# The first stage of a two-block network by pairs of K-blocks, with its early modulation in pieces of 256 columns

## The chip, the cores and the metric

The kernel runs on one core of one Trainium2 chip. The metric is the device time of one execution in microseconds (us), as the median of several runs of the same program; lower is better. A core has five engines that run their own instruction streams: TensorE (PE in the profile, with its weight loads apart as PEld), VectorE (DVE), ScalarE (ACT), GpSimd (POOL) and SyncE (SP), which here issues all loads from memory.

## The reference

Two blocks of layers over 256 tokens of width 1024, batch 1. What matters here is the beginning of the first layer, which treats the sequence `x` and a context `ctx` of 256 tokens alike:

```python
mod   = silu(c)     @ w_ada[0] + b_ada[0]        # 6*1024 columns: sh1, sc1, g1, sh2, sc2, g2
mod_c = silu(c_ctx) @ w_ada[0] + b_ada[0]
h  = rms_norm(x,   norm_mix[0]) * (1 + sc1)  + sh1
hc = rms_norm(ctx, norm_mix[0]) * (1 + sc1c) + sh1c
b_gate, c_gate, u = split(h @ conv_w_in, 3)      # 3 x 1024 columns; the same for hc
y = (b_gate * conv3(c_gate * u)) @ conv_w_out    # three taps along the tokens
```

The rest of the layer (gates g1 and g2, a SwiGLU layer), an attention layer and a second block of four feed-forward layers and two mixers follow. All of it is computed in float32 accuracy.

## The kernel before

Activations lie transposed: 128 features on the partitions, `KB` = 8 blocks of 128 features ("K-blocks"), and 512 columns, 256 tokens of x beside 256 of ctx. A float32 product is made of three matmuls of a faster type: each operand is split into a high part (rounded, by ScalarE) and a low part (the rest, by VectorE), and `mm3` (L241) adds high x high, high x low and low x high in one PSUM bank. In the profile these three are L243, L244 and L245.

Weights come as a stream of units (`WeightStream`, L67). A unit is up to 1024 columns per partition, here 2 K-blocks x 512 columns or 4 K-blocks x 256 columns (512 KB). There are 5 raw buffers, into which SP loads the units in the order of `stream_specs` (L698), and 4 buffers each for the high and the low parts. `take` (L111) splits up to two units ahead of the one it hands out (L106 on ScalarE, L107 on VectorE, in pieces of 512 columns); a load waits until its raw buffer has been split, or for an unsplit unit until it has been used.

Each engine executes its instructions in a fixed order. This order is made when the program is built: it follows the text, but an instruction whose inputs the builder takes to be ready may be put ahead of others that are not. So the text below gives priorities rather than the exact order.

The first stage is in `conv_block` (L759). X and ctx are loaded (L1784, L802), squared and summed (`squares`, L341), and `diagonal` makes the statistics: 8 matmuls against a vector of 1/D per 256 tokens (L361), a chain of some ten small VectorE steps that ends in the reciprocal root, and a diagonal matrix (L782). `normalise` spreads it over the partitions with one matmul (L787) and multiplies (L789), into `xr`.

The modulation vectors of the first layer's shift and scale are 2048 columns, made in four chunks of 512 (`ADA_FIRST`: chunks 0, 2, 1, 3; chunks 0 and 1 are the shift, 2 and 3 the scale). For all four chunks the 2 or 4 columns of silu(c) are the stationary operand and the weights move. Chunks 0 and 2 go by `ada_direct` (L446): the raw float32 weights, 8 matmuls of 512 columns each (L455). Chunks 1 and 3 go by `ada_fast` (L409): split weights against split silu columns, 16 matmuls of 512 columns each (L418, L419). The result is a row of 512 columns on 2 or 4 partitions; it is copied out of PSUM by ScalarE (L460, L424), turned into columns by four small transposes (L441, L428), and the bias is added (L444, or L432 to L435).

With chunks 0 and 2 the shift and scale of K-blocks 0 to 3 are there, and `modulate(0)` makes these four blocks of the convolution's input: `mod_scale` (L515), then for each block two ScalarE instructions (L798), a cast and a subtraction (L251, L252 into `xh` and `xl`). PE then adds these four K-blocks for the first four output blocks (two of c_gate, two of u, `pcu`). Chunks 1 and 3 and `modulate(1)` give the other four K-blocks. The two output blocks of b_gate follow with all eight K-blocks (L842). Group 0 is thus 6 output blocks x 8 K-blocks x 3 = 144 matmuls of 512 columns; three more groups like it follow. After each group VectorE and ScalarE take the banks out: a copy (L847), the product (L849), the three taps (L851 to L853), the gate (L855) and a split. Then `ada_at` starts the modulation of a later piece by VectorE alone (`ada_slow`, L476 and L478).

PSUM has 8 banks. `banks(5, 3)` (L194) makes 5 main banks for the blocks and 3 auxiliary banks, which the statistics, the spread diagonal and the modulation use. A bank is handed on tile by tile.

## Time and profile before

| what | us |
|---|---|
| runs (3): median | 2060.99 |
| runs: lowest and highest | 2060.79, 2061.44 |
| the profiled execution | 2061.66 |
| its span, first to last instruction | 2059.9 |
| TensorE busy in the span | 2022.4 |
| VectorE busy | 1522.6 |
| ScalarE busy | 1062.4 |

The page of the profile has the busy time of each engine, first over the span and then in slices. The trace behind it can be asked for busy time in chosen stretches, for instructions in order of time, for groups of instructions by tile or line, and for who waited for whom. A line of the order of time reads: start, duration, engine, line of the code, operation, written tile <- read tiles, shape, count, and in brackets how long the engine stood idle before it and what ended that. Where several equal instructions follow one another they are one line, and its duration runs from the first start to the last end. Loads are attributed to SP's queue. The granted clock is the share of full speed that TensorE got.

### The profile page before, as it was taken

To read this page: it belongs to the slowest core of one execution; us is meant where nothing else is said; L and a number is where in the kernel's file an instruction comes from. 1 tells how busy PE (TensorE), PEld (TensorE's weight loads), DVE (VectorE), ACT (ScalarE), POOL (GpSimd) and SP (SyncE) were. 2 spreads that over 40 slices of the span, in tenths; PEclk is the share of its full clock that TensorE was granted. 3 is DMA by queue.
4 is the path that set the end of the run, shared out by engine and by line. 5 is a ranking of instruction groups with operands and counts; after the bars stand their busy time and mean duration, and the time that the engine had idled before them with its cause. 6 is when DMAs were issued, how large, how long until landed. Compare 5 with 4: busy or idle time off the path is not lost. (4 is left out here: it accounts for less than half of the span.)

```text
span 2059.9 us, 32409 instructions
## 1 busy us (share of the span) xinstructions
PE 2022.4 (98%) x12430; PEld 1776.4 (86%) x12430; DVE 1522.6 (74%) x2796; ACT 1062.4 (52%) x1763; POOL 4.1 (0%) x24
## 2 busy tenths in 40 slices
PE   7999999999999999999999999999999999999999
PEld 3888887888899999888888889998888888989888
DVE  6979998766377778766677667787767776887774
ACT  4534533323355566555455546555545554675552
POOL 0000000000000000000000000000000000000000
PEclk9999999999999999999999999999999999999999
DMA  7746566656254324466566564556656656425554
GB/s 249 230 144 195 174 206 197 219 189 200 89 165 148 98 88 137 138 186 188 180 190 186 178 189 137 151 171 189 189 176 192 185 183 190 138 83 166 186 180 133
DMA packets 327434, 350.93 MB, mean 170 GB/s; under 512 B 12592, under 2 KB 301488, under 8 KB 327280
## 3 DMA queue, kind: packets, MB, share of 16 engines
q1 hardware_dynamic: 327280, 348.88, 54.8%
q8 instruction: 97, 1.59, 0.3%
q14 instruction: 57, 0.47, 0.1%
HBM read 347.78 MB, written 1.05 MB: 169 GB/s over the span
## 5 line engine op out<-in xcount | busy, mean ns | idle before, releaser
L106 ACT CAST whi<-wraw 128x512 fp32r<-128x512 f32 (+1 forms) x803 | 617.0, 791 | 713.0 <-issue 245.4
L107 DVE TENSOR_TENSOR wlo<-wraw,whi 128x512 fp32r<-128x512 f32 (+1 forms) x803 | 709.5, 900 | 343.5 <-ACT whi L106 340.5
L306 PE MATMUL pg<-x,whi 128*128 128x512 f32 x1408 | 387.9, 397 | 0.5 <-DVE x L255 0.3
L306 PEld LDWEIGHTS pg<-x,whi 128*128 128x128 f32 x1408 | 241.0, 188 | 33.9 <-DVE x L255 2.8
L306 PE MATMUL po<-s,whi 128*128 128x512 f32 x880 | 243.0, 394 | 0.0
L308 PEld LDWEIGHTS pg<-x,wlo 128*128 128x128 f32 x1408 | 215.1, 188 | 31.8
L308 PE MATMUL pg<-x,wlo 128*128 128x256 f32 x1408 | 223.3, 280 | 0.0
L243 PE MATMUL pm<-xh,whi 128*128 128x512 f32 (+1 forms) x576 | 217.2, 381 | 2.8 <-ACT xh L251 2.8
L244 PE MATMUL pm<-xl,whi 128*128 128x512 f32 (+1 forms) x576 | 218.4, 380 | 0.0
L245 PE MATMUL pm<-xh,wlo 128*128 128x512 f32 (+1 forms) x576 | 217.9, 379 | 0.0
L478 DVE SCALAR_TENSOR_TENSOR ada_acc<-wraw,sil,ada_acc 128x512 f32<-128x512 f32 x224 | 159.6, 751 | 24.0 <-DMA wraw<-in_w_ada 22.6
L306 PEld LDWEIGHTS po<-s,whi 128*128 128x128 f32 x880 | 148.7, 189 | 18.0
L308 PEld LDWEIGHTS po<-s,wlo 128*128 128x128 f32 x880 | 137.5, 188 | 20.5
L308 PE MATMUL po<-s,wlo 128*128 128x256 f32 x880 | 142.5, 280 | 0.0
L243 PEld LDWEIGHTS pm<-xh,whi 128*128 128x128 f32 x576 | 109.1, 190 | 25.7 <-ACT xh L251 4.1
L244 PEld LDWEIGHTS pm<-xl,whi 128*128 128x128 f32 x576 | 109.5, 190 | 20.6 <-DVE xl L252 0.2
L245 PEld LDWEIGHTS pm<-xh,wlo 128*128 128x128 f32 x576 | 109.2, 190 | 20.5
L245 PE MATMUL pm<-sh,wlo 128*128 128x256 f32 (+1 forms) x384 | 119.3, 311 | 0.7 <-DVE wlo L107 0.7
L243 PE MATMUL pm<-sh,whi 128*128 128x256 f32 (+1 forms) x384 | 119.2, 311 | 0.0
L244 PE MATMUL pm<-sl,whi 128*128 128x256 f32 (+1 forms) x384 | 118.9, 310 | 0.0
L245 PE MATMUL pm<-whi,xl 128*128 128x256 f32 x352 | 99.7, 283 | 0.0
L306 PE MATMUL pg<-xh,whi 128*128 128x512 f32 x352 | 96.1, 394 | 0.0
(435 smaller groups left out, 3467.4 us busy)
## 6 DMA issues: line engine op xcount, KB each, us to landing
wraw<-in_ffn_w_in SPq DMA_DIRECT2D x264, 512.0 KB, 3.6
wraw<-in_ffn_w_out SPq DMA_DIRECT2D x128, 512.0 KB, 3.5
wraw<-in_w_ada SPq DMA_DIRECT2D x96, 512.0 KB, 4.5
wraw<-in_a_w_in SPq DMA_DIRECT2D x28, 512.0 KB, 3.8
wraw<-in_conv_w_in SPq DMA_DIRECT2D x24, 512.0 KB, 4.7
wraw<-in_attn_w_qkv SPq DMA_DIRECT2D x24, 512.0 KB, 4.0
wraw<-in_conv_w_out SPq DMA_DIRECT2D x16, 512.0 KB, 4.3
wraw<-in_ffn_w_out SPq DMA_DIRECT2D x28, 256.0 KB, 2.7
```

The lines of the kernel that those rows point to most:

```text
L106: self.nc.scalar.copy(hi[:, cs], raw[:, cs])
L107: self.nc.vector.tensor_tensor(lo[:, cs], raw[:, cs], hi[:, cs].bitcast(F32), ALU.subtract)
L243: mm(ps, ah, bh, start=first, stop=False)
L244: mm(ps, ah, bl, start=False, stop=False)
L245: mm(ps, al, bh, start=False, stop=last)
L306: self.nc.tensor.matmul(pss[c], hi[:, kk, cs], x2[:, done + kk], start=done + kk == 0, stop=False)
L308: self.nc.tensor.matmul(pss[c][:, 0, :], lo[:, kk, cs], x2[:, done + kk, 0, :], start=False, stop=done + kk == nblocks - 1)
L478: nc.vector.scalar_tensor_tensor(accs[v], w[:, kk, :], c, accs[v], ALU.mult, ALU.add)
```

## The change

The four chunks of 512 columns become four pieces, one for each pair of K-blocks: 256 columns of the shift and the 256 columns of the scale that belong to them.

- Piece 0 (`ada_whole`) has its weights loaded outside the stream, into two tiles of 8 x 256 columns. Here the raw float32 weights are the stationary operand and the two silu columns move: 4 column blocks x 8 K-blocks = 32 matmuls, whose results lie on the partitions already, so that only the bias is added.
- Pieces 1 to 3 (`ada_parts`) go as `ada_fast` did, with 32 matmuls of 256 columns each, in place of 16 of 512.
- The convolution of group 0 goes by pairs: for each pair of K-blocks, the six output blocks (c_gate, u, b_gate, two each) are all advanced by these two K-blocks, in six banks that stay open over the four pairs. Its units are 2 K-blocks x 256 columns (256 KB). In the text, the next piece's matmuls stand behind the pair's c_gate blocks, its copy, transposes and `modulate` behind the first u block.
- PSUM is `banks(6, 2)` until group 0 is taken out, then `banks(5, 3)` as before.
- X is the first load, ahead of the two tables `pack` and `consts`. Then come half of piece 0, ctx, the other half of piece 0, and five units of the stream (before: two units, ctx, and the others as buffers came free).

```diff
-        self.banks(5, 3)
+        self.banks(6, 2)
+        self.X = self.cp.tile([P, KB, T], F32, name="X")
+        self.load_halves(self.X, a["xT"])
         self.pk = self.cp.tile([P, NPACK], F32, name="pk")
...
+    def mod_blocks(self, i):
+
+        m = self.mod[:, 0, 0:16, :].rearrange("p (s b) v -> p s b v", s=2)[:, :, 2 * i : 2 * i + 2, :]
+        bias = self.p("b_ada0")[:, 0:16].rearrange("p (s b) -> p s b", s=2)[:, :, 2 * i : 2 * i + 2]
+        return m, bias[:, :, :, None].to_broadcast([P, 2, 2, 2])
+
+    def ada_whole(self, w):
+
+        sil = self.sil.rearrange("p (v k) -> p k v", v=2)
+        ps = self.aux_bank()
+        m, bias = self.mod_blocks(0)
+        for s in range(2):
+            for c in range(2):
+                o = 4 * s + 2 * c
+                for kb in range(KB):
+                    self.nc.tensor.matmul(ps[:, o : o + 2], w[s][:, kb, c * P : (c + 1) * P], sil[:, kb, :], start=kb == 0, stop=kb == KB - 1)
+                if c == 0:
+                    yield
+            self.nc.vector.tensor_tensor(m[:, s], ps[:, 4 * s : 4 * s + 4].rearrange("p (b v) -> p b v", b=2), bias[:, s], ALU.add)
+
+    def ada_parts(self, i):
 
         nc = self.nc
         ps = self.aux_bank()
+        for s in range(2):
+            o = ps[0:4, s * 256 : (s + 1) * 256]
+            for h in range(2):
+                hi, lo, nk, _ = self.ws.take()
+                for kk in range(nk):
+                    kb = 4 * h + kk
+                    nc.tensor.matmul(o, self.c4[:, kb, :], hi[:, kk, :], start=kb == 0, stop=False)
+                    nc.tensor.matmul(o, self.c4[:, kb, :], lo[:, kk, :], start=False, stop=kb == KB - 1)
         row = self.tmp()
         nc.scalar.copy(row[0:4, :], ps[0:4, :])
         yield
         pt = self.aux_bank()
         for b in range(4):
             nc.tensor.transpose(pt[:, 4 * b : 4 * b + 4], row[0:4, b * P : (b + 1) * P], self.ident[0:4, 0:4])
...
+        m, bias = self.mod_blocks(i)
+        for s in range(2):
+            nc.vector.tensor_tensor(m[:, s], cv[:, s, :, :, 0], cv[:, s, :, :, 1], ALU.add)
+            nc.vector.tensor_tensor(m[:, s], m[:, s], bias[:, s], ALU.add)
...
+CONV_COLS = (1024, 2048, 0)
...
-    for i in range(2):
-        s += ada_units(w[0], ADA_FIRST[i], ADA_FIRST[i] in ADA_DIRECT)
-    for k0 in (0, 4):
-        for c0 in (1024, 2048):
-            s += cols_units(a["conv_w_in"], c0, 256, k8[k0 : k0 + 4])
-        if k0 == 0:
-            for i in range(2, 4):
-                s += ada_units(w[0], ADA_FIRST[i], ADA_FIRST[i] in ADA_DIRECT)
+    for i in range(4):
+        for n, c0 in enumerate(CONV_COLS):
+            s += cols_units(a["conv_w_in"], c0, 256, k8[2 * i : 2 * i + 2])
+            if n == 0 and i < 3:
+                for c1 in (0, 1024):
+                    s += cols_units(w[0], c1 + (i + 1) * 256, 256, k8)
...
+    w0 = [ep.tile([P, KB, 256], F32, name=f"ada{s}") for s in range(2)]
...
-    net.ws.load(2)
-    net.load_halves(net.C, net.a["ctxT"])
+    for s in range(2):
+        net.load_halves(w0[s], net.a["w_ada"][0][:, 1024 * s : 1024 * s + 256])
+        if s == 0:
+            net.load_halves(net.C, net.a["ctxT"])
+    net.ws.load(5)
+    ada = net.ada_whole(w0)
     dx = diagonal(0)
-    units(0, 2)
+    next(ada)
     normalise(0, dx)
     dc = diagonal(1)
-    units(0, 2)
+    next(ada)
     normalise(1, dc)
-    units(1, 4)
-    units(0, 1)
-    units(1, 1)
+    for _ in ada:
+        pass
     modulate(0)
...
+    pcu = [[net.main_bank() for _ in range(2)] for _ in CONV_COLS]
+    for i in range(4):
+        ada = None
+        for n, pss in enumerate(pcu):
+            hi, lo, nk, _ = net.ws.take()
+            for c in range(2):
+                cs = slice(c * P, (c + 1) * P)
+                for kk in range(nk):
+                    kb = 2 * i + kk
+                    net.mm3(pss[c], hi[:, kk, cs], lo[:, kk, cs], xh[:, kb, :], xl[:, kb, :], kb == 0, kb == KB - 1)
+                if n == 1 and c == 0 and ada is not None:
+                    for _ in ada:
+                        pass
+                    modulate(i + 1)
+            if n == 0 and i < 3:
+                ada = net.ada_parts(i + 1)
+                next(ada)
     early.close()
...
+                if g == 0:
+                    net.banks(5, 3)
                 net.ada_at("conv", g)
```

More of the change, by code (lines that the diff above doesn't have):

```diff
@@ L444, in ada_columns @@
         self.nc.vector.tensor_tensor(m, pt[:, :8].rearrange("p (b v) -> p b v", b=4), bias, ALU.add)
-    def ada_direct(self, layer, j):
-        nc = self.nc
-        ps = self.aux_bank()
-        sil = self.sil.rearrange("p (v k) -> p k v", v=2)
-        done = 0
-        while done < KB:
-            w, _, nk, _ = self.ws.take()
-            for kk in range(nk):
-                nc.tensor.matmul(ps[0:2, :], sil[:, done + kk, :], w[:, kk, :], start=done + kk == 0, stop=done + kk == KB - 1)
-            done += nk
-            if done < KB:
-                yield
-        row = self.tmp()
-        nc.scalar.copy(row[0:2, :], ps[0:2, :])
-        yield
-        self.ada_columns(layer, j, row)
     def ada_slow(self, layer, j, vecs):
@@ L667, in ffn_pairs @@
         self.ws.width = 512
-ADA_FIRST = (0, 2, 1, 3)
-ADA_DIRECT = (0, 2)
+CONV_COLS = (1024, 2048, 0)
 ADA_AT = {
@@ L767, in conv_block @@
     early = ExitStack()
-    xr = early.enter_context(tc.tile_pool(name="xr", bufs=1)).tile([P, KB, 512], F32, name="xr")
-    chunk = {j: net.ada_direct(0, j) if j in ADA_DIRECT else net.ada_fast(0, j) for j in ADA_FIRST}
-    def units(i, n):
-        for _ in range(n):
-            next(chunk[ADA_FIRST[i]], None)
+    ep = early.enter_context(tc.tile_pool(name="early", bufs=1))
+    xr = ep.tile([P, KB, 512], F32, name="xr")
+    w0 = [ep.tile([P, KB, 256], F32, name=f"ada{s}") for s in range(2)]
     def diagonal(v):
@@ L790, in normalise, with modulate @@
                                     R[:, None, :].to_broadcast([P, 2, T]), ALU.mult)
-    def modulate(half):
-        net.mod_scale(0, 0, half)
+    def modulate(i):
+        net.mod_scale(0, 0, i, 2)
         a = net.modA[:, 0, :, :]
-        for kb in range(4 * half, 4 * half + 4):
+        for kb in (2 * i, 2 * i + 1):
             t = net.tmp()
```

63 lines of the change are left out of this document (17 added, 46 removed).

## The prediction

> **What bounds the kernel now.** I read the page's head first, then busy time by stretches of the span, then the order of time up to 80 us, the only part that the diff touches.
>
> ```profile
> span 2059.9 us, 32409 instructions
> PE 2022.4 (98%) x12430; PEld 1776.4 (86%) x12430; DVE 1522.6 (74%) x2796; ACT 1062.4 (52%) x1763; POOL 4.1 (0%) x24
> ```
> ```profile
> 0.00:37.70 37.70, 22.65 (x64) 7.18 (x64) 20.40 (x60) 13.11 (x26) 0.21 (x4) 0.95 0.83 272
> 37.70:77.30 39.60, 39.59 (x170) 28.76 (x171) 34.09 (x61) 28.19 (x54) 0.00 (x0) 0.96 0.69 222
> ```
>
> PE is busy for 98% of the span. The second fence (columns: stretch, length, then busy time of PE, PEld, DVE, ACT and POOL, then granted clock, DMA share, GB/s) shows that up to 37.7 us PE has 15 us idle, and that from there it is never idle. All later stages are the same code. So the change is worth what it does to one moment: the time at which PE has done the 144 convolution matmuls of group 0 (6 output blocks x 8 K-blocks x 3) and the matmuls of the four early modulation chunks. That moment now:
>
> ```profile
> L243 PE MATMUL pm<-xh,whi x49: 387/389/796, 37.7 to 79.7; 128*128 128x512 f32 x49
> ```
>
> The 49th of the L243 matmuls, the first beyond the 48 of group 0, starts at 79.7 and each step of three takes 0.7, so the moment is about 79.1 us. (Some matmuls of other groups may be among the 49; the count of work is the same.) What set the start at 37.7 is in the order of time:
>
> ```profile
> 8.71 1.15 ACT L347 ACTIVATE t<-X 128x512 f32<-128x512 f32 x2 [0.27 <-DMA X<-in_xT]
> ...
> 10.92 1.87 PE L361 MATMUL pa<-mean,acc 128*128 128x1 f32 x8 [10.92 <-DVE acc L352]
> ...
> 14.37 1.15 ACT L347 ACTIVATE t<-C 128x512 f32<-128x512 f32 x2 [0.34 <-DMA C<-in_ctxT]
> ...
> 14.99 0.48 DVE L782 TENSOR_SCALAR t<-kc,rcol 128x128 f32<-128x128 f32 x2
> ...
> 15.91 2.29 DVE L352 TENSOR_TENSOR acc<-acc,t 128x512 f32<-128x512 f32 x3
> ...
> 18.22 0.70 PE L787 MATMUL pa<-t,ones 128*128 128x256 f32 x2
> ...
> 18.75 0.95 PE L361 MATMUL pa<-mean,acc 128*128 128x1 f32 x8
> 18.95 2.48 DVE L789 TENSOR_TENSOR xr<-X,pa 128x512 f32<-128x512 f32 x4 [0.76 <-PE pa L787]
> ...
> 24.84 2.48 DVE L789 TENSOR_TENSOR xr<-C,pa 128x512 f32<-128x512 f32 x4 [0.85 <-PE pa L787]
> ...
> 33.34 0.62 ACT L106 CAST whi<-wraw 128x512 fp32r<-128x512 f32 x1 [0.92 <-DMA wraw<-in_w_ada]
> ...
> 33.86 0.57 ACT L460 COPY t<-pa 2x512 f32<-2x512 f32 x1
> ...
> 34.48 0.58 PE L441 MATMUL pa<-kc,t 2*128 2x2 f32 x4 [2.38 <-ACT t L460]
> ...
> 35.56 1.59 ACT L798 ACTIVATE t<-xr,mod,modA 128x256 f32<-128x256 f32 x3 [0.61 <-DVE modA L515]
> ...
> 37.06 0.60 ACT L251 CAST xh<-t 128x512 fp32r<-128x512 f32 x1
> ...
> 37.72 2.08 PE L243 MATMUL pm<-xh,whi 128*128 128x512 f32 x4 [0.85 <-ACT xh L251]
> ```
>
> The normalised data xr is complete at 27.3, ten us before the first convolution matmul. The last thing to come is the second modulation chunk: its row copy (L460, 33.86), transposes, the first L798. So the chunks bind the start, and half of all modulation (4.2 MB of weights) must pass before it.
>
> **The change, part by part.** *Loads.* SP now issues X (1.05 MB), pack and consts (0.54), the first 256 columns of the shift (1.05), C (1.05), the first 256 columns of the scale (1.05), then five stream units (0.26 and 4 x 0.52), none of which waits for a buffer.
>
> ```profile
> 14.00:16.00 2.00, 2.00 (x3) 0.25 (x2) 1.72 (x9) 1.17 (x3) 0.00 (x0) 1.00 1.05 386
> ```
>
> C's end has the same 3.7 MB up to it as before, so it lands at 14.3 as now (the second squares start at 14.37). At 386 GB/s the scale's columns land 2.7 later, at 17.1, the first convolution unit at 17.8, the four units of the next piece at 19.1, 20.5, 21.8 and 23.2. X no longer has 0.54 MB ahead of it: 1.4 earlier, so its second half is there at 7.3.
>
> *Modulation of pair 0 with stationary weights.* 32 matmuls, fp32 128x128 loads and two moving columns. The nearest rows are the two L361 rows, fp32 128x128 loads with one moving column: 0.23 each in one, 0.12 in the other. That is 16 x 0.23 = 3.7 after 17.1, so 20.8 at the dear end, and the additions and L515 end near 21.5. No row copy, no transposes. It lies beside the ctx chain, which ends later, so it costs nothing; if C came 5 us earlier it would be what is late.
>
> *What is late next: xr of ctx.* x: sums at 9.5 (now 10.9), L361 to 11.4, then as now from 12.8 to 15.5 the small DVE steps, so 14.1; L787 0.7 and xr from 14.9. The ctx sums (from 15.5, 2.29 of DVE) and the x normalisation (2.48) now fall on the same engine: together done at 14.9 + 4.8 = 19.7. There are two auxiliary banks instead of three, one of them held by the modulation sums, so the ctx statistics (L361) also wait until xr of x has read its bank; that wait ends inside the same 19.7. Behind it on PE stand only modulation matmuls. From L361 to xr of ctx now takes 18.75 to 24.84, 6.1, and up to 0.9 more if its eight matmuls run at 0.23; then 0.7 for the first xr piece: 26.5 to 27.4. One L798 (0.53) and one cast (0.6) with their hand-overs, 1.25: the first convolution matmul at 27.7 to 28.7. I take **28.0**, so the start comes **9.7 earlier**.
>
> *PE work behind the start.*
>
> ```profile
> 50.76 0.40 PE L419 MATMUL pa<-wlo,c 128*4 128x512 f32 x1
> 51.00 0.39 PE L418 MATMUL pa<-whi,c 128*4 128x512 f32 x1
> ...
> 54.30 0.41 PE L428 MATMUL pa<-kc,t 4*128 4x4 f32 x4
> ...
> 217.20 0.28 PE L243 MATMUL pm<-sh,whi 128*128 128x256 f32 x1
> 217.32 0.28 PE L244 MATMUL pm<-sl,whi 128*128 128x256 f32 x1
> ```
>
> The convolution matmuls are the same 144. Before, 28 of the 32 L418/L419 matmuls lie behind the start, at 0.235 from start to start: 6.6, and two sets of transposes, 0.8: 7.4. After, each of three pieces has 32 matmuls of 256 columns at 0.12: 3.8. Piece 1 (landed 19.1 to 23.2, split before the start but for the last unit, since the four split buffers also hold the first convolution unit) leaves 8 x 0.12 = 1.0; pieces 2 and 3 are 7.7; transposes 3 x 0.41 = 1.2. Sum 9.9, so **2.5 more**. If none of piece 1 ran early it would be 5.3 more, if all did, 1.5.
>
> *The pair boundaries.* Each later pair's input follows from its piece: last matmul, row copy, transposes, six small DVE steps, two L798, cast. The trace has this chain once, between busy neighbours:
>
> ```profile
> 53.08 0.39 PE L419 MATMUL pa<-wlo,c 128*4 128x512 f32 x1
> 53.51 0.58 ACT L424 COPY t<-pa 4x512 f32<-4x512 f32 x1
> ...
> 59.30 0.53 PEld L243 LDWEIGHTS pm<-xh,whi 128*128 128x128 f32 x3 [0.26 <-ACT xh L251]
> ```
>
> From 53.47 to 59.30 it takes 5.8. In the written order 24 convolution matmuls of pair i stand behind the piece:
>
> ```profile
> 66.35 0.39 PE L243 MATMUL pm<-xh,whi 128*128 128x512 f32 x1
> 66.58 0.39 PE L244 MATMUL pm<-xl,whi 128*128 128x512 f32 x1
> ```
>
> At 0.23 they cover 5.4. So PE waits about 0.5 at each of three boundaries, **1.5**. Between zero (the piece's matmuls need no xh and may run earlier) and, in the rival below, 2.4 each. The transposes wait for the row copy with 6 convolution matmuls (1.4) in front of them; behind them on PE stand the next convolution matmuls, so a late copy holds up those.
>
> *The clock.* The start itself falls in a slow stretch now, and I leave it the same after:
>
> ```profile
> 33.50:34.00 0.50, 0.00 (x0) 0.00 (x0) 0.01 (x1) 0.50 (x2) 0.00 (x0) 0.79 0.95 287
> ...
> 37.70:40.70 3.00, 2.98 (x7) 2.41 (x8) 1.38 (x2) 3.00 (x7) 0.00 (x0) 0.51 0.68 264
> ```
>
> PE stood idle for 2.38 us before 34.48. In the half microsecond from 33.5 to 34, inside that gap, the granted clock is no longer 1.00 but 0.79 on the mean, and the first 3.0 us of convolution ran at 0.51, a loss of 1.5. The Trainium skill (TensorE: Matmul & The Clock Gate, "Why this matters for your kernels") asks for no idle gaps over about 3 us, since one idle window halves the clock. By that rule a gap of 2.4 us would go unpunished, which this trace contradicts; by it the third rival's price would lack its clock part and come out at 2061.
>
> *Edits at nothing.* The bank switch to (5, 3) after group 0: group 1 opens on banks 0 and 1, which L847 frees while the last 24 matmuls still run; if not, 0.6 for a copy. Six banks for group 0 remove a wait for a bank that PE does not show now.
>
> **Sum.** -9.7 + 2.5 + 1.5 = -5.7. The profiled execution took 2061.66 (span 2059.9 and 1.76 around it) and would take 2055.9; the median of the runs lies 0.67 below it, so **2055.3**.
>
> **Rivals.** *VectorE becomes the bound.*
>
> ```profile
> 60.00:100.00 40.00, 40.00 (x178) 32.97 (x177) 39.79 (x64) 17.59 (x33) 0.00 (x0) 1.00 0.67 204
> ```
> ```profile
> L107 DVE TENSOR_TENSOR wlo<-wraw,whi 128x512 fp32r<-128x512 f32 x32 | 20.8, 690 | 6.3 <-ACT whi L106 6.2
> ```
>
> DVE has no idle time from 60 to 100. Three split pieces instead of two chunks add 4 units x 2 x 0.69 = 5.5 to it, and PE arrives 5.7 earlier. If DVE's splits then bind, PE gives back 5.5: 2060.8. For it: that row. Against it: PE is never idle there now, and much of that DVE work is the slow modulation of later pieces, which nothing in group 1 waits for.
>
> *The start comes late.* The order on an engine is fixed: L460 above stood behind a cast that waited 0.92 for its DMA. If casts of the new units stand ahead of L798 or of the ctx squares in the same way, and the start is at 32, the sum is -1.7: 2059.3.
>
> *The boundaries are late and the clock falls (slower).* Each piece needs four units through four split buffers, while up to three of them hold convolution units of the pair that is still running. If the wait at each of three boundaries reaches the 2.38 us that halved the clock above, each costs 2.4 + 1.5: 11.7 in place of 1.5, so +4.5: 2065.5. It decides from the idle time at which the clock falls: at 1.4 (33.5 less 32.1, the gap's start) three waits with their slow stretches make 8.7, more than the 7.2 that start and PE work leave. For it: three serial chains where there were two. Against it: 12.5 us of PE work per pair (36 x 0.23 + 3.8 + 0.4) stand against 2.9 MB, 7.5 us of DMA at 386 GB/s, and PE did not wait through the chain at 53 to 59 now.
>
> **How the numbers follow.** Forecast 0.67 (0.64 faster by over 0.2%, 4.1 us, about what a measurement of this kernel can tell from no change; 0.03 within it); VectorE 0.12 and late start 0.10, both within 0.2%; boundaries 0.11, slower. So faster 0.64, same 0.25, slower 0.11. The forecast's own range: start 27.7, all of piece 1 early, no boundary waits, no slow stretch (-1.5): -10.0 - 1.5 + 1.5 = -10.0, so 2051.0; start 28.7, 24 of its 32 early, waits of 1 each: -9.0 + 2.5 + 3.0 = -3.5, so 2057.5. With the two middle rivals, and half a microsecond on either side for the spread of the runs (2060.79 to 2061.44), the range is 2050.5 to 2061.3; the slower one is left out.
>
> **What would show it.** Right: first L243 on pm near 28, L361 of ctx near 20, the 48 matmuls of each line done near 73, PE full from 28 on. Start late: first L243 past 31, with ACT L106 waiting for DMA in front. Boundaries: PE idle on ACT xh L251 near 37, 48 and 60, and granted clock 0.5 after it. VectorE: PE idle on wlo L107 or on banks between 72 and 100. Wrong altogether: a first matmul near 37, or the gain there at 80 us and gone by the end.

## The result, and the profile after

| | median us | lowest and highest |
|---|---|---|
| before | 2061.22 | 2060.79, 2063.57 |
| after | 2072.28 | 2071.70, 2073.80 |

The changed kernel takes 1.0056 times as long, 95% interval 1.0044 to 1.0067: 11.5 us more by that ratio, where 5.7 less was forecast. Its profiled run took 2071.7 us. Lines of the first stage have new numbers after the change: L361 is L366, L243 to L245 are L248 to L250, L251 and L252 are L256 and L257, L476 and L478 are L481 and L483; L429 are the matmuls of piece 0, L444 and L445 those of pieces 1 to 3.

The head of the page of the kernel after:

```profile
span 2069.9 us, 32649 instructions
PE 2029.3 (98%) x12522; PEld 1795.2 (87%) x12522; DVE 1528.1 (74%) x2815; ACT 1064.9 (51%) x1771; POOL 4.1 (0%) x24
```

Of the 10.0 us by which the span grew, 6.9 are PE time that counts as busy and 3.1 are idle. The moment that the prediction argued with, the end of group 0, is again given by the 49th L248 matmul (kernel after, operations of L248 up to 84.1 us):

```profile
L248 PE MATMUL pm<-xh,whi x49: 387/393/792, 35.2 to 83.8; 128*128 128x512 f32 x49
```

It was 79.7 before and is 83.8 now, so the stage is 4.1 later, although its first convolution matmul is 2.5 earlier (35.2 for 37.7). Why it is not 9.7 earlier is seen in the kernel after's order of time on PE:

```profile
9.72 1.87 PE L366 MATMUL pa<-mean,acc 128*128 128x1 f32 x8 [9.72 <-DVE acc L357]
11.45 6.97 PE L429 MATMUL pa<-sil,ada 128*128 128x2 f32 x32
18.27 1.20 PE L787 MATMUL pa<-t,ones 128*128 128x256 f32 x2
19.27 6.83 PE L429 MATMUL pa<-sil,ada 128*128 128x2 f32 x32
25.95 1.84 PE L366 MATMUL pa<-mean,acc 128*128 128x1 f32 x8
31.59 1.19 PE L787 MATMUL pa<-t,ones 128*128 128x256 f32 x2 [3.80 <-DVE t L782]
...
35.20 1.22 PE L248 MATMUL pm<-xh,whi 128*128 128x512 f32 x2 [0.49 <-ACT xh L256]
```

Piece 0 has 32 matmuls in the code and 64 records here: an fp32 matmul is two records. They take 6.97 + 6.83 = 13.8 us, 0.216 each. The first 32 stand ahead of the spread of x (L787), whose diagonal was ready at 14.26 (VectorE's L782, 13.78 + 0.48); the spread runs at 18.27. The second 32 stand ahead of the statistics of ctx (second L366 row), whose sums were ready at 24.72 (L357, 22.43 + 2.29). So the chain of x and ctx, which was forecast to be the late one with piece 0 beside it, runs behind piece 0.

The rest of the loss comes later. Kernel after, busy time by stretches (columns as in the prediction):

```profile
60.00:100.00 40.00, 38.84 (x184) 29.91 (x183) 35.05 (x61) 23.92 (x44) 0.00 (x0) 1.00 0.63 197
35.20:40.50 5.30, 5.30 (x13) 3.86 (x14) 4.92 (x9) 2.75 (x6) 0.00 (x0) 1.00 0.20 59
180.00:200.00 20.00, 15.56 (x85) 12.75 (x84) 19.45 (x33) 9.86 (x18) 0.00 (x0) 0.86 0.56 178
195.00:199.40 4.40, 3.80 (x15) 3.35 (x15) 4.12 (x8) 1.43 (x3) 0.00 (x0) 0.50 0.30 86
```

The same 20 us in the kernel before:

```profile
180.00:200.00 20.00, 20.00 (x158) 18.06 (x158) 19.86 (x39) 11.97 (x24) 0.00 (x0) 1.00 0.57 179
```

From 60 to 100 PE is idle for 1.2 us and VectorE for 5, so VectorE is no longer full there. From 180 to 200 PE lacks 4.4 us; before the change it was busy for all 20. In these 20 us the convolution's output product (conv_out) begins. What PE waits for there (kernel after, order of time on PE):

```profile
190.90 0.39 PE L248 MATMUL pm<-sh,whi 128*128 128x256 f32 x1 [0.62 <-ACT sh L256]
191.62 0.39 PE L249 MATMUL pm<-sl,whi 128*128 128x256 f32 x1 [0.34 <-DVE sl L257]
...
195.03 0.58 PE L248 MATMUL pm<-sh,whi 128*128 128x256 f32 x1 [2.90 <-ACT sh L256]
196.18 0.58 PE L249 MATMUL pm<-sl,whi 128*128 128x256 f32 x1 [0.57 <-DVE sl L257]
```

It waits for sh and sl, the two parts of the gated product of the last two output blocks of group 3, which VectorE makes late. The granted clock after the gap of 2.90 is 0.50, and matmuls of 256 columns are 0.21 apart there instead of 0.12. Compared matmul by matmul, the kernel after is 4.05 behind at the end of group 0, 5.2 behind from the middle of group 1 to the end of group 3, 12.9 behind in most of the first half of conv_out and 11.0 behind in its second half; by the end this has shrunk to 10.1. So 4 us are lost in the first stage, 1 in group 1, and some 6 at the entry of conv_out.

VectorE's last gated product, with its low part sl, ends at 196.1 instead of 185.4. Up to there VectorE is busy for 154.2 us (148.3 before) and idle for 41.9 (37.1 before). The busy part that grew is the weight splits (L107): 80 of 0.686 us, 54.9 in all, for 72 of 0.689, 49.6 in all.

### The profile page after: what moved, and what is told of

It reads as the page before. It is cut to its first block, busy times and chain, and to the rows that moved or that the text cites. A ratio compares the mean times of both kernels' runs of the same rounds, so it can differ in the third digit from the quotient of the medians.

```text
span 2069.9 us, 32649 instructions
## 1 busy us (share of the span) xinstructions
PE 2029.3 (98%) x12522; PEld 1795.2 (87%) x12522; DVE 1528.1 (74%) x2815; ACT 1064.9 (51%) x1771; POOL 4.1 (0%) x24
## 3 DMA queue, kind: packets, MB, share of 16 engines
q8 instruction: 98, 1.61, 0.3%
## 5 line engine op out<-in xcount | busy, mean ns | idle before, releaser
L107 DVE TENSOR_TENSOR wlo<-wraw,whi 128x512 fp32r<-128x512 f32 (+1 forms) x811 | 713.8, 895 | 340.4 <-ACT whi L106 337.4
L248 PE MATMUL pm<-xh,whi 128*128 128x512 f32 (+1 forms) x576 | 217.9, 382 | 2.4 <-ACT xh L256 2.4
L249 PE MATMUL pm<-xl,whi 128*128 128x512 f32 (+1 forms) x576 | 219.2, 381 | 0.3 <-DVE xl L257 0.3
L250 PE MATMUL pm<-xh,wlo 128*128 128x512 f32 (+1 forms) x576 | 218.7, 380 | 0.8 <-DVE wlo L107 0.8
L483 DVE SCALAR_TENSOR_TENSOR ada_acc<-wraw,sil,ada_acc 128x512 f32<-128x512 f32 x224 | 159.3, 746 | 25.4 <-DMA wraw<-in_w_ada 23.7
L311 PEld LDWEIGHTS po<-s,whi 128*128 128x128 f32 x880 | 148.7, 189 | 18.1
L248 PEld LDWEIGHTS pm<-xh,whi 128*128 128x128 f32 x576 | 108.9, 190 | 25.0 <-ACT xh L256 3.8
L249 PEld LDWEIGHTS pm<-xl,whi 128*128 128x128 f32 x576 | 109.6, 190 | 21.4 <-DVE xl L257 1.7
L250 PEld LDWEIGHTS pm<-xh,wlo 128*128 128x128 f32 x576 | 109.5, 190 | 21.3 <-DVE wlo L107 1.2
L248 PE MATMUL pm<-sh,whi 128*128 128x256 f32 (+1 forms) x384 | 120.1, 313 | 3.5 <-ACT sh L256 3.5
L249 PE MATMUL pm<-sl,whi 128*128 128x256 f32 (+1 forms) x384 | 119.7, 312 | 0.9 <-DVE sl L257 0.9
L250 PE MATMUL pm<-sh,wlo 128*128 128x256 f32 (+1 forms) x384 | 119.7, 312 | 0.0
L250 PE MATMUL pm<-whi,xl 128*128 128x256 f32 x352 | 99.6, 283 | 0.0
```

Of the source, the lines that this page charges most:

```text
L107: self.nc.vector.tensor_tensor(lo[:, cs], raw[:, cs], hi[:, cs].bitcast(F32), ALU.subtract)
L248: mm(ps, ah, bh, start=first, stop=False)
L249: mm(ps, ah, bl, start=False, stop=False)
L250: mm(ps, al, bh, start=False, stop=last)
L311: self.nc.tensor.matmul(pss[c], hi[:, kk, cs], x2[:, done + kk], start=done + kk == 0, stop=False)
L483: nc.vector.scalar_tensor_tensor(accs[v], w[:, kk, :], c, accs[v], ALU.mult, ALU.add)
```

## The experiments

Each kernel was timed beside the kernel before on the same chip; ratios are to that, with 95% intervals. The first theory: piece 0's form costs the first stage some 4 us, and VectorE's added work costs the rest.

**e1_moving** makes piece 0 with moving weights, as the direct chunks were made, and leaves the rest of the change:

```
-  matmul(ps[:, o:o+2], w[s][:, kb, c*P:(c+1)*P], sil[:, kb, :], ...)       # 32, two columns each
+  matmul(ps[0:2, s*256:(s+1)*256], sil[:, kb, :], w[s][:, kb, :], ...)      # 16, 256 columns each
+  row copy and four transposes
```

> The changed kernel with one thing undone: piece 0 goes with moving weights again (the two silu columns stationary, raw float32 weights in 256 columns, then row copy, four transposes, bias). In the changed kernel's trace piece 0 stands as two groups of 32 matmuls, 6.97 and 6.83 us, in front of the spread of x (L787, ready at 14.3, run at 18.3) and of the ctx statistics (ready at 24.7, run at 26.0). Theory A (the start is late because these matmuls are twice as many as I counted and block PE's queue): two groups of 16 at 0.21 to 0.43, so 3.5 to 4.5 us each; first convolution matmul between 29 and 32 instead of 35.2, and the end 3 to 6 earlier, 2066 to 2069. Theory B (what costs is the pair structure after the start: more PE work and VectorE's lag): the first matmul comes earlier, but less than 2 us of it is left at the end, about 2071.

Measured: 1.0034 (1.0021 to 1.0047), about 2068. Piece 0 now takes 9.3 us on PE; the spread of x is at 16.8 and that of ctx at 26.5. The first convolution matmul comes only at 35.0, not between 29 and 32: 22 of the 96 matmuls of pieces 1 to 3 now run ahead of it, 9 in the kernel after. Group 0 ends 0.1 earlier than before the change and 4.2 earlier than in the kernel after. Of these 4.2, 1.5 are matmuls of the pieces that no longer lie behind the start, and 2.3 are convolution matmuls, which run at full speed nearly from the start on (on this part see "The clock" below). The wait at conv_out is the same 4.4, so it does not depend on the form of piece 0.

**e2_nopiece** leaves piece 0's matmuls out:

```
-  ada_whole: matmuls, then m = sums + bias
+  m = bias
```

> The changed kernel without the modulation of piece 0: shift and scale of K-blocks 0 and 1 are the bias alone, its weights are loaded but no matmul reads them (so this part of the computation is left out). It bounds what any form of piece 0 can be worth. Theory A: PE is free for the spread of x at 14 and for the ctx statistics near 20; first convolution matmul at 27 to 29, where I had forecast it, and the end 6 to 8 earlier than the changed kernel, about 2065, which is still 4 slower than the kernel before. Theory B: the start comes there too, but the end moves by less than 3, about 2070, since VectorE sets the rest of the convolution.

Measured: 1.0027 (1.0018 to 1.0036). The first convolution matmul is at 30.7, 7.0 earlier than before the change, yet group 0 ends only 0.6 earlier. Even a free piece 0 would not have brought the forecast. Behind the start PE spends 3.2 us more than before the change on matmuls of the pieces (83 of the 96 lie there) and 0.3 more on transposes, and it is idle for 2.9, mostly in two waits for the input of a later pair (1.79 at 42.6, 1.10 at 69.7).

**e3_slow_first** moves chunk 4 (the first of the slow chunks, those that VectorE multiplies) in the stream and in the text ahead of the fourth pair:

```
+  if i == 3: s += ada_specs(w, "conv", 0)         # ahead of the pair's loads
+  if i == 3: net.ada_at("conv", 0)
```

> The changed kernel with the first slow modulation (chunk 4, by VectorE alone) moved in the stream and in the text from behind group 0 to in front of pair 3. In the changed kernel VectorE begins it at 72.6 instead of 59.9, and is 10.8 late at the end of the convolution, where PE waits 4.4 us for it and then runs 5 us at half clock. Theory B (VectorE's lag comes from the late start of its slow work): it begins at 58 to 62, the wait near 190 is gone, and the end is 5 to 7 earlier, about 2066; the start at 35.2 stays. Theory A (all of the loss is PE's late start and its work): the wait near 190 stays in some form and the end moves by less than 2.

Measured: 1.0040 (1.0025 to 1.0054). Group 0 ends 8.7 later than before the change, since PE waits 1.8 and 3.4 us for inputs of the pairs; but at conv_out PE waits only 0.8. So the wait at conv_out hangs on when chunk 4 is done relative to PE, not on how late the stage is.

**e4_later** moves chunk 7 from behind group 3 to behind the second group of conv_out:

```
-  ("conv", 3): [(0, 7)], ("conv_out", 0): [(0, 8)]
+  ("conv_out", 0): [(0, 8)], ("conv_out", 1): [(0, 7)]
```

> The changed kernel with the slow modulation of chunk 7 moved from behind convolution group 3 to behind the second group of the output product, so that VectorE has less to do just before the output product begins. If the wait for the split of the gated product at 190 to 196 is VectorE's queue (theory B), it vanishes and the end is 4 to 6 earlier, about 2067, unless the moved work makes PE wait later by as much. If that wait is the tail of the convolution itself (banks, the taps' chain), it stays and the end moves by less than 1.

Measured: 1.0051 (1.0036 to 1.0066). The wait at conv_out falls from 4.4 to 1.0, but PE is idle for 2.6 between 204 and 250 where the kernel after has none. The lateness is moved, not paid off.

**e5_split_more** puts the suspected VectorE work into the kernel before:

```
-  ADA_DIRECT = (0, 2)
+  ADA_DIRECT = (0,)
```

> The kernel before, in which the second early modulation chunk (2) is split into high and low parts instead of multiplied unsplit: eight more subtractions on VectorE, 8 x 0.69 = 5.5 us, as many as the change adds; load order and pair structure stay as before. Theory (the added split work makes VectorE late at the entry of conv_out, where it has no slack): PE waits for sh/sl near 185 to 192 for 3 to 5 us, time 2061 + 4 = about 2065. Rival (the half-filled buffers and the order of the loads make VectorE late, not its work): no wait there, 2059 to 2062.

Measured: 0.9995 (0.9986 to 1.0003), with 80 splits up to the last gated product as in the kernel after, and PE idle for 0.3 at conv_out. The theory of the added split work falls.

**e6_raw_piece** takes it out of e1_moving: piece 3 is multiplied unsplit.

```
-  cols_units(w[0], c1 + 3*256, 256, k8)           # split, 32 matmuls
+  cols_units(w[0], c1 + 3*256, 256, k8, raw)      # unsplit, 16 fp32 matmuls
```

> e1_moving, with the last piece (K-blocks 6 and 7) multiplied unsplit in fp32: eight subtractions fewer on VectorE, so as many as before the change; on PE 32 records of 256 fp32 columns in place of 32 faster ones, estimated 2 to 4 us more. Theory (split work): the wait of 4.7 at the entry of conv_out falls to under 1 and so does the 1.5 near k60 to k72: 2067 - 4 - 1 + 3 = about 2065, stage end (48 of each line) 2 to 4 later than e1_moving. Rival (load order): the wait stays and PE's part adds: 2070.

Measured: 1.0043 (1.0031 to 1.0056), 72 splits, PE idle for 4.1 at conv_out. VectorE up to the last gated product is busy for 148.7 and idle for 45.9 (e1_moving: 154.0 and 38.2): what was saved in work became waiting. That agrees with e5_split_more.

**e7_pool** gives the 24 low parts of pieces 1 to 3 in e1_moving to GpSimd:

```
-  nc.vector.tensor_tensor(lo, raw, hi, subtract)
+  nc.gpsimd.tensor_tensor(lo, raw, hi, subtract)   # pieces' units only
```

> e1_moving, with the 24 low-part subtractions of pieces 1 to 3 done by GpSimd, which is idle: 24 x 0.69 = 16.6 us less on VectorE. Theory (VectorE's work): no wait at the entry of conv_out, 2067 - 6 = 2061 or less if GpSimd takes under 2 us for one 128x512 subtraction; if it takes 3 us, a piece's 8 take 24 us and the pairs wait: stage end 10 or more later and 2070 or more. Rival (load order): the wait stays, 2066 to 2068.

Measured: 1.0086 (1.0072 to 1.0099). GpSimd's work (groups of instructions, kernel e7_pool):

```profile
L108 POOL TENSOR_TENSOR wlo<-wraw,whi 128x512 fp32r<-128x512 f32 x24 | 33.6, 1429 | 40.4 <-ACT whi L106 40.4
```

One takes 1.43 us, on VectorE 0.69 with GpSimd idle, so a piece's eight take 11.4, the pairs wait, and group 0 ends 11.7 later than before the change. The Trainium skill (GPSIMD Engine Reference, "Elementwise — side-by-side cycle accounting") has GpSimd about two times slower on a tensor_tensor; the ratio here is 2.08 (1.43 to 0.69). PE still waits 4.0 at conv_out. But VectorE was not relieved, so this run does not test its work: what VectorE does while GpSimd works takes longer. Of these two equal steps only the second falls into GpSimd's time, which begins at 37.65 (kernel e7_pool, order of time on VectorE):

```profile
36.59 0.69 DVE L258 TENSOR_TENSOR xl<-t,xh 128x512 fp32r<-128x512 f32 x1 [2.22 <-ACT xh L257]
38.13 1.38 DVE L258 TENSOR_TENSOR xl<-t,xh 128x512 fp32r<-128x512 f32 x1 [0.84 <-ACT xh L257]
```

Up to its last gated product VectorE is busy for 154.5 us with 56 splits, in e1_moving for 154.0 with 80.

**e8_behind** changes only the order in the text of the changed kernel:

```
   dx = diagonal(0)
+  normalise(0, dx)
   next(ada)
-  normalise(0, dx)
   dc = diagonal(1)
+  normalise(1, dc)
   next(ada)
-  normalise(1, dc)
```

> The changed kernel with only the written order turned round: the spread of the x statistics stands ahead of the first half of piece 0's matmuls, and the statistics and spread of ctx ahead of the second half. Theory (both the queue and PE's own 13.8 us of piece 0 cost): x spread at 14.3 in place of 18.3, ctx statistics near 22.5 in place of 26, second half of piece 0 behind the ctx spread and 6.9 long, first convolution matmul 33 to 34.5 in place of 35.2, so no more than 2 us gained: 2070 to 2072. Rival (the queue alone: piece 0 costs nothing once it stands behind): first convolution matmul near 30, 2067.

Measured: 1.0072 (1.0060 to 1.0085). x is spread at 14.2 as expected, but the builder put both halves of piece 0 ahead of the statistics of ctx, so that ctx is spread at 35.3 and the first convolution matmul is at 38.9. The forecast of 2070 to 2072 missed, and the run does not separate queue from duration. e11_behind2 does.

**e9_halves** halves, in the kernel before, the loads of group 0 ahead of chunk 4, to test a second theory: the five raw buffers, half filled, cover half the PE work, so chunk 4 is loaded late.

```
-  cols_units(conv_w_in, c0, 256, 4 K-blocks)
+  two of cols_units(conv_w_in, c0, 256, 2 K-blocks)      # K-blocks 4 to 7 of c_gate and u, all of b_gate
```

> The kernel before, with the eight convolution loads ahead of the first slow modulation chunk (chunk 4) cut to half size, as the change cuts them (K-blocks 4 to 7 of the first two columns and all of the third in units of two K-blocks): same bytes, same splits, same PE work, no other edit. New theory (the loads run five buffers ahead; with half-filled buffers that is half the PE work, so chunk 4 starts about 11.5 us before the end of group 0 and not 19 to 23, VectorE never catches up, and PE waits for sh/sl at the entry of conv_out): chunk 4's first step near 67 in place of 59.9, PE idle of about 4 near 185 to 190 with a slow stretch behind it, 2061 + 5 = about 2066. Rival (something else in the pair structure makes VectorE late): chunk 4 near 60 to 63, no wait, 2060 to 2062.

Measured: 1.0011 (1.0003 to 1.0020). Chunk 4 starts at 65.6 instead of 59.9, as expected, but PE is idle for only 0.8 at conv_out: by chunk 7 VectorE has made the delay up (140.7, before the change 140.8). Chunk 4 is 13.5 us ahead of the end of group 0 here, not the 11.5 expected, so this run is not as late as the pair kernels with 11.4.

**e10_joined** is e1_moving with pairs 2 and 3 made one:

```
-  for i in range(4): K-blocks 2i, 2i+1; piece i+1 inside pair i
+  for i in range(3): K-blocks (0, 1), (2, 3), (4 to 7); piece 1 inside the first, 2 and 3 inside the second
```

> e1_moving with pairs 2 and 3 joined: pieces 2 and 3 come together inside pair 1, and K-blocks 4 to 7 follow as three full-size loads, so full buffers stand ahead of chunk 4. Theory (lookahead): chunk 4's first step 19 to 23 before the end of group 0 as in the kernel before, not 11.4; no wait of 4.4 at the entry of conv_out. Stage end 0 to 3 later than e1_moving, since eight piece loads must pass inside one pair. Time 2067 - 6 + 2 = about 2063. Rival (pairs as such or the split work): the wait of 2.9 stays, 2067 to 2069.

Measured: 1.0001 (0.9991 to 1.0010). Group 0 ends 1.7 later than in e1_moving, but PE is idle for only 0.8 at conv_out (kernel e10_joined, the same stretch):

```profile
180.00:200.00 20.00, 19.24 (x145) 16.72 (x143) 19.90 (x39) 11.15 (x22) 0.00 (x0) 1.00 0.53 176
```

**e11_behind2** puts all of piece 0 in the changed kernel behind both normalisations:

```
   dx = diagonal(0); normalise(0, dx); dc = diagonal(1); normalise(1, dc)
+  next(ada); next(ada)
```

> The changed kernel with all of piece 0's stationary matmuls written behind the normalisation of x and of ctx, so that they stand behind both spreads on PE. Theory (PE spends 13.8 us on piece 0, 64 records at 0.21, wherever it stands): x spread 14.2, ctx spread near 26 in place of 31.6, then the 64 records, first convolution matmul near 41 to 43, 2074 to 2079. Rival (the place in the queue alone costs, the matmuls are worth about 4 us): first convolution matmul 30 to 32, 2066 to 2068.

Measured: 1.0087 (1.0073 to 1.0100). Kernel e11_behind2, order of time on PE:

```profile
14.19 1.22 PE L787 MATMUL pa<-t,ones 128*128 128x256 f32 x2 [2.73 <-DVE t L782]
20.80 1.83 PE L366 MATMUL pa<-mean,acc 128*128 128x1 f32 x8 [5.39 <-DVE acc L357]
26.43 1.19 PE L787 MATMUL pa<-t,ones 128*128 128x256 f32 x2 [3.80 <-DVE t L782]
27.42 6.83 PE L429 MATMUL pa<-sil,ada 128*128 128x2 f32 x32
...
34.50 6.99 PE L429 MATMUL pa<-sil,ada 128*128 128x2 f32 x32
```

The chain of x and ctx alone runs nearly as the prediction had it: x spread at 14.2 (forecast 14.1), ctx statistics at 20.8 (20), ctx spread at 26.4. Piece 0 then takes its 13.8 us in the open. The first convolution matmul comes at 46.8, later than the 41 to 43 expected, because 26 matmuls of piece 1 run in between. So both halves of the prediction's step were wrong: the 32 matmuls take 13.8, where its rate gives 7.4, and in none of the three places tried in PE's order (kernel after, e8_behind, e11_behind2) are they hidden.

**e12_joined_only** joins pairs 2 and 3 in the changed kernel (the edit of e10_joined) and leaves the stationary weights.

> The changed kernel with pairs 2 and 3 joined as in e10_joined, and piece 0 still with stationary weights: one of the two causes undone. Theory (two independent losses, about 5 from piece 0's form in the first stage and about 6 from the shortened run of loads): no wait of 2.9 at the entry of conv_out, chunk 4's first step 16 or more before the end of group 0, stage end 4 to 7 later than in the kernel before, time about 2066. Rival (the wait at conv_out follows from the late stage end, not from the loads): the wait stays and the time is 2072 or more.

Measured: 1.0011 (1.0002 to 1.0020), so 9.3 of the 11.5 us are gone with this edit alone. Group 0 ends 3.0 later than before the change, and at conv_out PE is idle for only 0.1 (kernel e12_joined_only):

```profile
180.00:200.00 20.00, 19.91 (x145) 17.11 (x144) 19.90 (x38) 10.74 (x22) 0.00 (x0) 1.00 0.57 178
```

**e13_halves_split** has both edits of e5_split_more and e9_halves in the kernel before, in case the wait takes both.

> The kernel before with both additions at once, the half-size loads of e9_halves and the eight more splits of e5_split_more; each alone cost 0 to 3. Theory A (half-filled buffers and the added split work cost only together: VectorE is sent off late and has no slack left to make it up): the waits of 2.9 and more at the entry of conv_out appear, 2065 to 2068. Theory B (neither matters much; the place of the pieces in the run of loads does): no such wait, 2060 to 2063.

Measured: 0.9991 (0.9982 to 1.0000), PE idle for 0.1 at conv_out, with chunk 4 at 14.0 ahead of the end of group 0. Theory A falls.

**e14_joined_halves** is e10_joined with the loads of K-blocks 4 to 7 at half size:

```
-  cols_units(conv_w_in, c0, 256, K-blocks 4 to 7)
+  cols_units(conv_w_in, c0, 256, K-blocks 4, 5) + cols_units(conv_w_in, c0, 256, K-blocks 6, 7)
```

> e10_joined with the loads of K-blocks 4 to 7 cut to half size: same order of work on PE and same pieces inside pair 1, but six half-filled loads ahead of chunk 4 in place of three full ones. Theory A (half-filled buffers): chunk 4's first step 12 to 14 before the end of group 0 in place of 17.3, wait of 3 to 4 at the entry of conv_out, 2064 to 2067. Theory B (what counts is that no piece stands among the last loads): wait under 1, 2060 to 2062.

Measured: 1.0004 (0.9995 to 1.0012), PE idle for 1.2 at conv_out and no gap of 2.9. Theory B's time came, and its wait (under 1) nearly. Chunk 4 is 16.4 ahead, not the 12 to 14 of theory A: half-size loads alone did not make it late here, so the run does not show what a late chunk 4 would have done in this kernel.

Together, in us against the kernel before. The time is 2061 times (ratio - 1), good to about 2 or 3 us by its interval; the other columns are from one trace each. Chunk 4's lead is from its first step to the end of group 0, chunk 7's from its first step to conv_out's first matmul. The end of group 0 is taken as the first low-part matmul (L244 and L249) behind it.

| kernel | time | end of group 0 | time less that | chunk 4's lead | chunk 7's lead | PE idle 181 to 204 |
|---|---|---|---|---|---|---|
| before | 0 | 0 | 0 | 20.1 | 40.4 | 0 |
| after | +11.5 | +4.1 | +7.4 | 11.4 | 35.2 | 4.4 |
| e1_moving | +7.0 | -0.1 | +7.1 | 11.4 | 35.0 | 4.4 |
| e2_nopiece | +5.6 | -0.6 | +6.2 | 11.4 | 34.5 | 4.8 |
| e6_raw_piece | +8.9 | +2.8 | +6.1 | 12.2 | 35.5 | 4.1 |
| e7_pool | +17.7 | +11.7 | +6.0 | 12.2 | 35.6 | 4.0 |
| e8_behind | +14.8 | +7.1 | +7.7 | 11.5 | 35.1 | 4.3 |
| e11_behind2 | +17.9 | +10.6 | +7.3 | 11.4 | 35.4 | 4.2 |
| e3_slow_first | +8.2 | +8.7 | -0.5 | 20.4 | 39.9 | 0.8 |
| e5_split_more | -1.0 | -1.0 | 0.0 | 23.1 | 40.3 | 0.3 |
| e9_halves | +2.3 | -0.9 | +3.2 | 13.5 | 39.7 | 0.8 |
| e10_joined | +0.2 | +1.6 | -1.4 | 17.3 | 39.4 | 0.8 |
| e12_joined_only | +2.3 | +3.0 | -0.7 | 17.5 | 40.1 | 0.1 |
| e13_halves_split | -1.9 | -0.8 | -1.1 | 14.0 | 40.3 | 0.1 |
| e14_joined_halves | +0.8 | -0.1 | +0.9 | 16.4 | 38.9 | 1.2 |

(e4_later, where chunk 7 is elsewhere, is at +10.5, +3.5 and +7.0.) There are two kinds. Where piece 3 stands inside pair 2 and chunk 4 behind pair 3, chunk 4's lead is 12.2 or less and conv_out costs 6 to 8 us, whatever the stage before it does. Where the last pieces are out of the way or chunk 4 goes ahead, the lead is 13.5 or more and PE waits for 1.2 at most; the 3.2 of e9_halves stands out, but its time is good to 1.8 either way, and matmul by matmul its trace has lost 1.6 there. The changed kernel pays both: 4.1 in the stage and 7.4 behind it. No version beats the kernel before by more than can be told apart here.

## Why the prediction was wrong, point by point

**Piece 0 "costs nothing".** This step failed first. The prediction priced each matmul at the rate of an L361 row, "16 x 0.23 = 3.7" for the 16 matmuls behind the last load. But a row counts records, and these fp32 matmuls are two records each. L361's eight records are four matmuls in the code (two blocks of 128 tokens, two halves of the sums), not eight as the description of the kernel says, and the kernel before has 32 records of L455 for the 16 matmuls of chunks 0 and 2. This row alone is half of them:

```profile
24.74 7.03 PE L455 MATMUL pa<-wraw,sil 128*2 128x512 f32 x16
```

At two records per matmul the same 0.23 gives 7.4 for the 16 matmuls, where 6.83 was measured, and 14.7 for all 32, where 13.8 was. The second slip is that of place: "beside the ctx chain" was true of its data, not of PE's fixed order, where the 64 records stand ahead of L787 and of the second L366. e11_behind2 shows the first slip alone. In the times, e2_nopiece without these matmuls is at +5.6 and the kernel after at +11.5.

**Loads and the ctx chain, first convolution at 28.0.** The loads landed as forecast as far as the chain shows (sums of x at 9.72, forecast 9.5), and e11_behind2 has x spread and ctx statistics at their forecast times within 0.8. Behind that the chain was priced too short. In e2_nopiece, with piece 0 free, three weight splits (L107, 0.7 each) stand between the small VectorE steps of ctx, xr of ctx begins at 28.2 with its first piece done at 28.9 (forecast 26.5 to 27.4), and the first convolution matmul is at 30.7. With piece 0 ahead it is at 35.2: 2.5 gained, not 9.7.

**PE work behind the start, 2.5.** The prediction wanted all of piece 1 but one unit ahead of the start. PE ran 9 of the 96 matmuls of pieces 1 to 3 before it; the first is at 32.2. From start to start of the matmuls the stage adds up: start 2.5 earlier, pieces' matmuls behind it 10.2 for 6.6, convolution matmuls 37.04 for 34.75, transposes 0.3 more, idle time 0.4 more: -2.5 + 3.6 + 2.3 + 0.3 + 0.4 = +4.1. The prediction had 5.3 as the price if none of piece 1 ran early, but gave that end no weight.

**Pair boundaries, 1.5.** In the kernel after PE's idle time from the start to the end of group 0 is only 0.4, but that looks like luck: PE ran slowly there (next point), so the next pair's input had more time. In e2_nopiece, e3_slow_first, e8_behind and e12_joined_only, which start the convolution at full speed with as little of piece 1 done, PE waits between 1.2 and 1.8 for xh at the first boundary alone, where 0.5 was forecast. The third rival had the right sign, but what it describes did not happen in the kernel after.

**The clock, "the same".** The first convolution matmuls ran at half speed for 5.3 us instead of 3.0, 0.43 apart in place of 0.23. That is 1.1 of the 2.3 above; the rest is a dozen slower steps of 0.32 to 0.41 later in the stage, where the kernel before has four. As far as these traces show, the long stretch is chance and not a price of the change. In e12_joined_only PE has the same work in the same order up to there, within 0.1 us of the same times, but then its convolution matmuls are 0.23 apart, and it does 31 matmuls of all sizes where the kernel after does 13 (kernel after, then e12_joined_only):

```profile
35.00:40.50 5.50, 5.30 (x13) 3.87 (x14) 5.12 (x9) 2.95 (x7) 0.00 (x0) 1.00 0.19 57
35.00:40.50 5.50, 5.32 (x31) 3.82 (x32) 5.50 (x10) 3.98 (x8) 0.00 (x0) 1.00 0.22 54
```

e4_later went slowly there as well, e3_slow_first at full speed. So a part of the 4.1 of the first stage, and of the 4.2 between the kernel after and e1_moving, hangs on it.

**Edits at nothing.** The bank switch and the six banks show no wait of PE; that held.

**"From there PE is never idle. All later stages are the same code. So the change is worth what it does to one moment."** This is the step that lost most. The later stages are the same code but not in the same phase: VectorE came out of the first stage late relative to PE, and the wait came 110 us further on, at 190. The VectorE rival saw that VectorE was full from 60 to 100, and sized the added splits well (5.5; 5.3 measured), but put the wait between 72 and 100, where PE lost about 1.1 (0.81 of it in a wait for wlo, L107, at 96), and took the time of before as the worst it could do. And its mechanism is wrong: e5_split_more, e6_raw_piece and e13_halves_split show that the split work is not what makes the wait.

What makes it, as far as shown: chunk 4 starts late. SP's queue loads it from 52.24 on in the kernel before, and VectorE begins it without a wait:

```profile
52.24 6.21 SPq L90 DMA_DIRECT2D wraw<-in_w_ada  x4
...
59.89 0.88 DVE L476 TENSOR_SCALAR ada_acc<-wraw,sil 128x512 f32<-128x512 f32 x2
```

In the kernel after it is loaded from 67.93 on, behind the loads of pair 3:

```profile
63.70 3.99 SPq L90 DMA_DIRECT2D wraw<-in_conv_w_in  x3
67.93 2.58 SPq L90 DMA_DIRECT2D wraw<-in_w_ada  x4
```

VectorE waits for it (kernel after, order of time on VectorE):

```profile
72.56 0.88 DVE L481 TENSOR_SCALAR ada_acc<-wraw,sil 128x512 f32<-128x512 f32 x2 [1.11 <-DMA wraw<-in_w_ada]
```

That is 11.4 us ahead of the end of group 0, where it was 20.1 (84.01 - 72.56 and 79.95 - 59.89). Joining the last pairs made it 17.3 and 17.5, moving chunk 4 made it 20.4; in these the wait at conv_out is gone. The delay is handed on whole: from chunk 4's first step to chunk 7's takes 78.8 us in the kernel after, 79.3 in e1_moving, and as much in the joined kernels (79.2 in e10_joined, 78.9 in e12_joined_only, 78.8 in e14_joined_halves), so what joining gains at chunk 4 is still there at chunk 7. That a late VectorE then doesn't catch up, though it has 5 us of idle time from 60 to 100 alone, is read from its order, not tested: chunk 7, in the kernel before,

```profile
137.06 14.78 SPq L90 DMA_DIRECT2D wraw<-in_w_ada  x4
...
140.85 0.88 DVE L476 TENSOR_SCALAR ada_acc<-wraw,sil 128x512 f32<-128x512 f32 x2 [3.82 <-DMA wraw<-in_w_ada]
```

and in the kernel after:

```profile
147.65 14.69 SPq L90 DMA_DIRECT2D wraw<-in_w_ada  x4
...
151.36 0.88 DVE L481 TENSOR_SCALAR ada_acc<-wraw,sil 128x512 f32<-128x512 f32 x2 [3.73 <-DMA wraw<-in_w_ada]
```

In both, the chunk's load is issued within 0.1 us of the end of a pair of splits on VectorE (135.74 + 1.29 and 146.34 + 1.29), which frees the raw buffer, and VectorE then stands idle for 3.8 until it lands. That idle time is a round trip through its own buffer, so it is as long when VectorE is late as when it is early. What stays open is why e9_halves and e13_halves_split, with chunk 4 only 13.5 and 14.0 ahead, made the delay up between chunks 5 and 7 (75.1 us from chunk 4 to chunk 7 in both) and the pair kernels did not. VectorE's order of chunk steps and evacuations, which the builder makes anew for each kernel, differs between them in that stretch; no run holds it fixed. Nor does a run move chunk 4's start and nothing else; e3_slow_first, which comes nearest, also makes the pairs wait.

## What to carry to other kernels

Count a row's records against the instructions in the code before its rate is used, and look up where the new instructions will stand in the engine's fixed order: work whose data is off the critical path can still stand in front of it. That the code behind the change is the same does not make its time the same: check every engine's phase against PE at the next stage whose input must be complete, not only PE's moment at the end of the changed one. When an engine that is full is suspected, add the suspected work to the kernel before: here that took one line and cleared it. And before a microsecond or two of a stage is put down to the change, see in a second trace whether PE ran at the same speed there.

## What the runs showed of the hardware

- An fp32 matmul is two records on PE here (64 for the 32 of piece 0, 32 for the 16 of chunks 0 and 2); the fp32 2x2 transposes are one. With 128x128 stationary weights and two moving columns a record took 0.216 us in the first 30 us of the span, about as much as one with one moving column in the first L361 row (1.87 / 8 = 0.23).
- The granted-clock column does not always show a slow PE: from 35.2 to 40.5 in the kernel after it reads 1.00 while matmuls of 512 columns are 0.43 apart instead of 0.23. The distance between equal matmuls does. That a stretch is slow can also be chance: e12_joined_only and e3_slow_first, with the same work up to there, ran it at full speed.
- Whether the clock falls does not follow from the length of one gap alone. Gaps of 1.21 (e1_moving, at 91.1), 1.61 (e8_behind, 50.9), 1.77 (e3_slow_first, 47.5) and 1.79 (e2_nopiece, 42.6), each between long stretches of large matmuls, were followed by matmuls at full speed. Gaps of 2.90 (kernel after, 192.1, with 0.62 and 0.34 of idle time just ahead of it) and 3.37 (e3_slow_first, 74.7) were followed by half speed, but so was one of 1.38 (e4_later, 209.1; granted clock 0.50 from 211.5 to 214), with four 2x2 transposes and another 0.20 of idle time just ahead of it. The Trainium skill (TensorE: Matmul & The Clock Gate, "Why this matters for your kernels") asks for no idle gaps over about 3 us. The 2.90 is at the edge of that rule and the 1.38 would pass by it, but half speed came behind both.
- VectorE can slow down while GpSimd works: in e7_pool a 128x512 subtraction took 1.38 us instead of 0.69 (shown above), and steps on 128x2 values took 1.18 to 1.23 at 24.8 to 28.5, in GpSimd's time, instead of 0.16.
